# Two-part score products for the heads, page-wise keys for the samples and two banks for branch products in a hybrid decoder step

## The chip, the cores and the metric

The kernel runs on one core of one Trainium2 chip. A core has TensorE (PE, matrix products, written to the eight banks of PSUM), VectorE (DVE), ScalarE (ACT), GpSimd (POOL) and SyncE (SP, which issues most of the transfers). The engines run beside each other, each takes its own instructions in order, and they wait for each other through semaphores. The metric is the device time of one execution in microseconds.

## What is computed

One step of a decoder layer, for 512 new prompt tokens and for 8 sequences of 4 sampled tokens each with 1024 cached positions (544 tokens in all). Everything comes in and goes out as float32. Cut to what matters:

```python
# one projection of the normed input gives all of these
q_a, kv_a, q_i, k_i, w_i, q_b, kv_b, gates = _project(_rmsnorm(x), w_in, pos)
# A: sparse attention, 8 heads on 2 key groups, the 256 best keys by an indexer score
s = einsum('btcgd,btncd->btcgn', q_a, keys_of(idx)) * HEAD_DIM ** -0.5 ; p = softmax(s)
# B: stick-breaking attention, 8 heads
z = einsum('bthd,bshd->bhts', q_b, k_b) * HEAD_DIM ** -0.5
a = exp(log_sigmoid(z) + sum of log(1 - sigmoid(z)) over the later keys) ; o_b = a @ v_b
merged = gates[0] * (o_a @ w_br_a) + gates[1] * (o_b @ w_br_b)
h = x + merged @ w_o ; h = h + _ffn(_rmsnorm(h)) ; y = _rmsnorm(h)
```

## The kernel before

The tokens are the columns of the products (two halves of 256 and 288 columns), so an activation is a tile of 128 features by 544 tokens. Dense products are made of two-part numbers: a value is split into a high part in the format float32r and the rest (`wh`, `wl` for weights, `xh`, `xl` for activations), and three products `wh*xh + wl*xh + wh*xl` are added in PSUM (L502, in `pieces`). For the weights the high part is an ACT copy (L113) and the low part a POOL subtraction (L117). The heads' and samples' products take plain float32, which PE issues as two rows of the trace for each product.

In order of time: the input is normed and turned; the indexer's rows, the stick-breaking queries, keys and values are projected (`V["wide"]`, banks in turn); from about 178 us three streams run beside each other in `beside`, each a generator that yields its estimated cost, the next step being taken from the stream that is least far along its given total (`S_COST`, `H_COST`, `D_COST`): *samples* (`sb_sample`, then `dsa_sample`), *heads* (`staged`: stick-breaking, then sparse, each over 4 pairs of heads j and 4 row blocks i, so 32 units) and *dense* (remaining projections and gates, then `branch_b`, which makes the first `NB` = 5 of 8 row blocks of the stick-breaking branch product). From about 485 us on there are only branch products, then the gates, `w_o` and the FFN. Within that program order a planner with a simulated timeline places each engine's instructions.

PSUM has 8 banks: `mm` 1, `z` 2, `acc` 1, `tp` 2, `ts` 2. A unit of the heads (`sb_first`, `dsa_first`) takes one tile `z` of two banks, one for each head of the pair, and makes both heads' scores side by side, each in a 64-row half of the array (`scores_of`, L859). In the stick-breaking branch a mask product (L935) is added, ACT makes two sigmoids (L938, L939), DVE a scan and a product (L941, L942); in the sparse branch DVE adds the mask (L972) and ACT takes the exponential. Queries and keys of a pair are loaded in `sb_load` and `dsa_load`, at i = 1 and i = 0 of the pair before.

In `sb_sample` the cached keys of four sequences at a time come by pages of 128 positions (`rows_of_page`, 12 tiles), are turned (L1030) and copied out of PSUM (`out_of`); `scores` (L1038) makes the logits of two pages in `acc`, which are copied to `zr`, from which `weights` takes the sigmoids. Outside the wide stages `pieces` uses the bank `mm` alone, and ACT copies it out (L538 for projections, L1281 for branch products) into `rowy`, of which there are two tiles.

## Time and profile before

| | us |
|---|---|
| median of 3 runs (range) | 994.39 (994.14 to 999.39) |
| profiled execution | 998.12 |
| its span, first to last instruction | 996.0 |
| PE busy in the span | 939.0 (94%) |
| DVE, ACT, POOL busy | 642.2, 452.5, 298.3 |

A row of the timeline gives the start and the duration of an instruction, or of several alike in a row (x4). Matmuls are pipelined and their ends are modelled, so the duration of a PE row runs on into the next row; what a product costs in a dense stretch is read from its start to the next start.

### The profile page before, as it was taken

How to read it: one execution, taken by the hardware profiler on the slowest of the kernel's cores; microseconds unless marked ns; L12 is line 12 of the kernel's file. 1: busy time of each engine (PE TensorE's matmuls, PEld its weight loads, DVE VectorE, ACT ScalarE, POOL GpSimd, SP SyncE). 2: the span in 40 equal slices, each digit the busy share in tenths (PEclk: the TensorE clock that was granted, in tenths of full speed). 3: DMA queues.
4: the chain of work that ended last, by engine and by line, in shares of the span. 5: the costliest groups of instructions: out<-in, count | busy, mean ns of one | idle time of the engine just before them, and what ended most of it. 6: DMA issues, size and time to landing. Idle time of an engine off the chain costs nothing.

```text
span 996.0 us, 19681 instructions
## 1 busy us (share of the span) xinstructions
PE 939.0 (94%) x7412; PEld 846.9 (85%) x7412; DVE 642.2 (64%) x1238; ACT 452.5 (45%) x889; POOL 298.3 (30%) x260
## 2 busy tenths in 40 slices
PE   5989999889899999999978999999999999999995
PEld 4989999766478775877768999989999999999995
DVE  4465999475565574443204585987778788875874
ACT  6214543455335434444555355544444445442453
POOL 3544343211221321223238456222322232201331
PEclk9989999989999999999999999999999999999998
DMA  9673454857787698415267845123333431235212
GB/s 262 179 191 107 132 159 140 263 164 216 243 256 229 201 305 261 151 61 223 88 209 231 229 116 146 46 64 107 86 102 89 123 90 41 66 93 160 83 48 90
DMA packets 180408, 150.67 MB, mean 151 GB/s; under 512 B 12378, under 2 KB 147354, under 8 KB 179290
## 3 DMA queue, kind: packets, MB, share of 16 engines
q1 hardware_dynamic: 175146, 134.45, 45.1%
q0 software_dynamic: 1872, 10.75, 3.1%
q10 hardware_dynamic: 3296, 4.23, 1.4%
q8 instruction: 58, 0.95, 0.4%
q14 instruction: 36, 0.29, 0.1%
HBM read 126.43 MB, written 17.56 MB: 145 GB/s over the span
## 4 chain that ended last, share of the span: by engine, by line
PE 66%; DVE 10%; DMA 8%; issue 3%; POOL 2%; ACT 2%; SPq 1%; ACTq 0%; DVEq 0%; POOLq 0%
PE mm L502 14%; PE ffB L1562 9%; PE ffC L1562 5%; PE ffA L1562 5%; PE ts L502 3%; PE ts L1647 3%; PE ts L1030 2%; PE z L859 2%; PE acc L502 2%; PE z L502 2%; PE dnB L1740 2%; PE tp L866 2%; POOL wl L117 2%; PE tp L875 1%; PE acc L1647 1%
## 5 line engine op out<-in xcount | busy, mean ns | idle before, releaser
L117 POOL TENSOR_TENSOR wl<-wst,wh 128x512 fp32r<-128x512 f32 (+2 forms) x136 | 161.3, 1209 | 307.4 <-ACT wh L113 293.1
L502 PE MATMUL mm<-xh,wh 128*128 128x256 f32 (+2 forms) x484 | 148.0, 306 | 9.4 <-ACT rowy L1281 7.1
L502 PE MATMUL mm<-xh,wl 128*128 128x256 f32 (+2 forms) x484 | 143.7, 297 | 1.3 <-POOL wl L117 1.3
L502 PE MATMUL mm<-xl,wh 128*128 128x256 f32 (+2 forms) x484 | 143.9, 297 | 0.0
L237 POOL TENSOR_TENSOR wl<-wst,wh 128x512 fp32r<-128x512 f32 (+1 forms) x48 | 66.7, 1410 | 174.0 <-ACT wh L234 157.9
L502 PEld LDWEIGHTS mm<-xh,wh 128*128 128x128 f32 (+1 forms) x484 | 93.4, 193 | 21.7 <-ACT rowy L1281 8.9
L113 ACT ACTIVATE wh<-wst 128x1024 fp32r<-128x1024 f32 (+3 forms) x83 | 75.1, 906 | 55.8 <-PE ts L1647 23.5
L502 PEld LDWEIGHTS mm<-xh,wl 128*128 128x128 f32 (+1 forms) x484 | 93.1, 192 | 7.7 <-issue 6.1
L502 PEld LDWEIGHTS mm<-xl,wh 128*128 128x128 f32 (+1 forms) x484 | 93.2, 192 | 2.0 <-issue 1.6
L234 ACT ACTIVATE wh<-ws 128x1024 fp32r<-128x1024 f32 (+1 forms) x55 | 54.9, 998 | 79.2 <-PE ffB L1562 29.2
L239 DVE TENSOR_TENSOR wl<-ws,wh 128x1024 fp32r<-128x1024 f32 (+1 forms) x55 | 66.4, 1208 | 5.5 <-ACT wh L234 5.5
L234 ACT ACTIVATE wh<-wst 128x1024 fp32r<-128x1024 f32 (+1 forms) x34 | 34.8, 1024 | 23.6 <-PE ffB L1562 15.5
L1030 PE MATMUL ts<-ident,kb 128*128 128x128 f32 x256 | 39.1, 282 | 2.1 <-DMA kb<-in_cache_kv_b 1.1
L843 ACT ACTIVATE kk<-ts 128x512 f32<-128x512 f32 x43 | 25.1, 600 | 31.4 <-PE ts L1030 31.0
L237 POOL TENSOR_TENSOR wl<-raw,wh 128x384 fp32r<-128x384 f32 x14 | 14.2, 1039 | 80.3 <-ACT wh L234 64.3
L538 ACT ACTIVATE rowy<-mm 128x256 f32<-128x256 f32 (+1 forms) x40 | 15.8, 394 | 49.3 <-PE mm L502 41.5
L1030 PEld LDWEIGHTS ts<-ident,kb 128*128 128x128 f32 x256 | 29.2, 144 | 7.7 <-DMA kb<-in_cache_kv_b 1.3
L211 DVE TENSOR_TENSOR ws<-wst 128x1024 f32<-128x1024 f32 (+1 forms) x11 | 21.4, 1947 | 19.9 <-DMA wst<-in_w_ffn_up 18.8
L1647 PE MATMUL ts<-actp,wh 128*128 128x288 f32 x160 | 34.1, 295 | 0.0
L941 DVE TENSOR_TENSOR_SCAN g<-g,z 128x128 f32<-128x128 f32 (+3 forms) x32 | 26.1, 816 | 11.8 <-ACT z L939 9.2
L938 ACT ACTIVATE g<-z 128x128 f32<-128x128 f32 (+3 forms) x32 | 13.9, 436 | 37.0 <-PE z L935 34.3
L502 PE MATMUL z<-xh,wh 128*128 128x288 f32 (+2 forms) x92 | 28.1, 305 | 1.8 <-DVE hT L1379 1.8
(485 smaller groups left out, 3075.4 us busy)
## 6 DMA issues: line engine op xcount, KB each, us to landing
wst<-in_w_in SPq DMA_DIRECT2D x38, 512.0 KB, 4.2
kb<-in_cache_kv_b SPq DMA_DIRECT2D x64, 256.0 KB, 3.8
vb<-in_cache_kv_b SPq DMA_DIRECT2D x64, 256.0 KB, 4.9
wst<-in_w_ffn_gate SPq DMA_DIRECT2D x40, 256.0 KB, 3.0
wst<-in_w_ffn_up SPq DMA_DIRECT2D x40, 256.0 KB, 3.4
wst<-in_w_ffn_down SPq DMA_DIRECT2D x16, 320.0 KB, 3.1
gate_d<-rowy SPq DMA_DIRECT2D x16, 272.0 KB, 2.1
gt<-gate_d SPq DMA_DIRECT2D x16, 272.0 KB, 3.6
```

Of the source, the lines that this page charges most:

```text
L113: self.nc.scalar.activation(h, st, AF.Copy)
L117: self.nc.gpsimd.tensor_sub(l[:, k], st[:, k], h[:, k].bitcast(F32))
L211: v.tensor_add(t, a("A21"), a("A22"))
L234: self.nc.scalar.activation(h, src, AF.Copy)
L237: self.nc.gpsimd.tensor_sub(l[:, g], src[:, g], h[:, g].bitcast(F32))
L239: self.nc.vector.tensor_sub(l, src, h.bitcast(F32))
L502: nc.tensor.matmul(ps, ww[:, k, :m], aa[:, k, hs], start=(k == 0 and p == 0), stop=(k == nk - 1 and p == 2))
L843: nc.scalar.activation(dst, ps, AF.Copy)
L941: nc.vector.tensor_tensor_scan(gr, gr, z[:, :n], 1.0, OP.mult, OP.bypass)
L1030: nc.tensor.transpose(tp[:, (2 * j + pg) * P:(2 * j + pg + 1) * P], raws[pg][:, (2 * jj + j) * P:(2 * jj + j + 1) * P], ident)
L1562: nc.tensor.matmul(ps[:, g], ww[:, g, k, :], aa[:, k, :], start=(first and k == 0 and p == 0), stop=(k == 3 and p == 2), skip_group_check= ...
L1647: nc.tensor.matmul(ps, ww[:, k - ks[0], :], aa[:, hs], start=(k + p == 0), stop=(k + 1 == DOWN[-1][-1] and p == 2))
```

## The change

The tile `z` becomes two tiles of one bank. A head's query tile holds its high part in the first 64 rows and its low part in the other 64, its key tile holds the keys' high parts in both halves and, in a second plane, their low parts in both; two products over all 128 rows with float32r operands then give the four partial products. The parts are made on chip from a raw tile that is loaded twice, once into each half. Loads for the next pair are issued at i = 3, head by head. The samples' keys are turned by single pages, the logits of half a sequence's keys (four pages) stay in `acc`, and the sigmoids read it there. Branch products in the overlapped stretch take `mm` and `acc` in turn. The bank lists of the other stages are adapted to the two `z` tiles, and costs, totals and buffer counts change.

```diff
-H_COST = 80
-D_COST = 174
+H_COST = 88
+D_COST = 185
-KV_C = 6
-KH_B = 8
+KV_C = 4
+KH_B = 6
-    zb2 = lambda: V["psum"].tile([P, 2, 512], F32, tag="z", name="z", bufs=1)
-    zb = lambda: zb2()[:, 0, :]
+    zb = lambda: bank("z", 2)
...
-    px_banks = cycle([lat, lts, lat, lts, zb, acc])
+    px_banks = cycle([lat, lts, lat, lts, zb, zb, acc])
...
-    V["banks"], many = cycle([mm, zb, acc, lts]), cycle([mm, zb, acc, lts, lts])
+    V["banks"], many = cycle([mm, zb, zb, acc]), cycle([mm, zb, zb, acc, lts, lts])
...
-            ps = (next(V["banks"]) if V["wide"] else mm)()[:m, :hs.stop - hs.start]
+            ps = (next(V["banks"]) if V["wide"] or nk == 4 else mm)()[:m, :hs.stop - hs.start]
...
-    def scores_of(zs, q, k, i):
+    def both_halves(pool, tag, src):
+
+        t = pool.tile([P, *src.shape[1:]], F32, tag=tag, name=tag, bufs=1)
+        for e in range(2):
+            nc.sync.dma_start(t[half_of(e)], src)
+        return t
+
+    def query_parts(pool, src, name):
+
+        t = both_halves(pool, "qraw", src)
+        q = pool.tile([P, T], F32R, tag="qq", name=name, bufs=2)
+        nc.scalar.activation(q, t, AF.Copy)
+        nc.vector.tensor_sub(q[64:], t[64:], S(q[64:]))
+        return q
+
+    def key_parts(pool, src, tag, bufs):
+
+        t = both_halves(pool, "kraw", src)
+        k = pool.tile([P, 2, T], F32R, tag=tag, name=tag, bufs=bufs)
+        nc.scalar.activation(k[:, 0], t, AF.Copy)
+        nc.gpsimd.tensor_sub(k[:, 1], t, S(k[:, 0]))
+        return k
 
+    def scores_of(z, q, k, i):
         n = (i + 1) * P
-        in_turn([lambda e=e: nc.tensor.matmul(zs[:, e, :n], q[half_of(e), i * P:(i + 1) * P], k[half_of(e), :n], start=True, stop=True,
-                                              skip_group_check=True) for e in range(2)])
+        for v in range(2):
+            nc.tensor.matmul(z[:, :n], q[:, i * P:(i + 1) * P], k[:, v, :n], start=(v == 0), stop=(v == 1))
...
     def sb_first(j, i):
-        if i == 1 and j < 3:
-            sb_load(j + 1)
-        q, kk, _ = V["sbq", j]
         n = (i + 1) * P
-        zs = zb2()
-        scores_of(zs, q, kk, i)
...
         for e in range(2):
-            z = zs[:, e]
+            z = zb()
+            scores_of(z, *V["sbq", 2 * j + e], i)
+            if i == 3 and j < 3:
+                sb_load(2 * j + 2 + e)
...
-        if i == 0 and j < 3:
-            dsa_load(j + 1)
...
+            z = zb()
+            scores_of(z, V["dsaq", 2 * j + e], kaa[j // 2], i)
+            if i == 3 and j < 3:
+                dsa_load(2 * j + 2 + e)
...
-        def scores(g, c, jj, kks, z):
-            for j in range(2):
-                side_by_side(lambda n4: nc.tensor.matmul(
-                    z[quarter(n4), :2 * P], qb[:, 4 * g + n4, 2 * jj + j, :], kks[n4][:, j, :],
-                    start=(jj + j == 0), stop=(jj + j == 2), skip_group_check=True))
+        def scores(g, c, kks, z):
+
+            in_turn([lambda j=j, n4=n4: nc.tensor.matmul(
+                z[quarter(n4), c * P:(c + 1) * P], qb[:, 4 * g + n4, j, :], kks[n4][:, j, :],
+                start=(j == 0 and c == 0), stop=(j == 3), skip_group_check=True) for j in range(4) for n4 in range(3, -1, -1)])
+
+        def logits(g, half):
+
+            z, ahead = acc(), []
+            for c in range(4):
+                kks = []
+                for n4 in range(4):
+                    kks.append(keys(rows_of_page(0, 4 * g + n4, 4 * half + c)))
+                    yield 0.45
+                    if n4 == 1 and ahead:
+                        scores(g, *ahead.pop(), z)
+                        yield 1.1
+                ahead.append((c, kks))
+            scores(g, *ahead.pop(), z)
+            yield 1.1
+            return z
...
-            nc.scalar.activation(r[:, lo:hi], zr[:, lo:hi], AF.Sigmoid, scale=-1.0)
-            nc.scalar.activation(zr[:, lo:hi], zr[:, lo:hi], AF.Sigmoid)
+            nc.scalar.activation(r[:, lo:lo + 512], z, AF.Sigmoid, scale=-1.0)
+            nc.scalar.activation(zr[:, lo:lo + 512], z, AF.Sigmoid)
+            if half:
+                nc.scalar.activation(r[:, PAST:], zr[:, PAST:], AF.Sigmoid, scale=-1.0)
+                nc.scalar.activation(zr[:, PAST:], zr[:, PAST:], AF.Sigmoid)
...
-    V["wide"] = False
+    V["wide"], V["banks"] = False, cycle([mm, acc])
...
-        kaa, va = dp.tile([P, 2, T], F32, name="kaa"), dp.tile([P, 4, P], F32, name="va")
-        for e in range(2):
-            nc.sync.dma_start(kaa[half_of(e)], ka_d.rearrange("(c d) t -> d c t", c=2))
+        kaa, va = [key_parts(dp, ka_d[half_of(c)], "kaa", 2) for c in range(2)], dp.tile([P, 4, P], F32, name="va")
...
-    V["banks"] = cycle([mm, lts, acc, lts])
+    V["banks"] = cycle([mm, zb, zb, acc])
```

## Rows read from the trace of the kernel before

**Rows 1.** The page's chain that ended last, share of the span by engine.
```profile
PE 66%; DVE 10%; DMA 8%; issue 3%; POOL 2%; ACT 2%; SPq 1%; ACTq 0%; DVEq 0%; POOLq 0%
```

**Rows 2.** Windows: busy us by engine (instructions), then granted clock, DMA share, GB/s.
```profile
178.00:330.00 152.00, 140.10 (x1163) 102.10 (x1164) 88.16 (x232) 71.42 (x161) 30.97 (x23) 0.97 0.74 229
485.00:530.00 45.00, 34.91 (x300) 28.94 (x300) 6.97 (x18) 23.79 (x46) 16.58 (x21) 1.00 0.54 170
...
200.00:225.00 25.00, 21.33 (x168) 15.42 (x167) 17.92 (x43) 14.17 (x32) 2.51 (x2) 0.86 0.51 166
```

**Rows 3.** Timeline of PE (start, duration, what): paired scores L859 and neighbours.
```profile
188.93 0.28 PE L502 MATMUL mm<-xh,wh 128*128 128x256 f32 x1
189.14 0.70 PE L859 MATMUL z<-kk,qq 64*128 64x256 f32 x4
...
243.02 1.13 PE L859 MATMUL z<-kk,qq 64*128 64x512 f32 x4
...
251.44 0.49 PE L859 MATMUL z<-kk,qq 64*128 64x128 f32 x4 [0.40 <-PE acc L1038]
...
433.17 1.13 PE L859 MATMUL z<-kaa,qqa 64*128 64x512 f32 x4
434.23 0.40 PE L502 MATMUL mm<-xh,wh 128*128 128x288 f32 x1
434.47 0.29 PE L502 MATMUL mm<-xh,wl 128*128 128x288 f32 x1
434.60 0.29 PE L502 MATMUL mm<-xl,wh 128*128 128x288 f32 x1
...
438.27 0.49 PE L859 MATMUL z<-kaa,qqa 64*128 64x128 f32 x4
438.70 0.76 PE L1006 MATMUL ts<-ident,sr 128*128 128x128 f32 x5
```

**Rows 4.** Timeline of PE: the prompt indexer's two-part scores, 256 and 512 keys.
```profile
88.17 0.28 PE L831 MATMUL tp<-kll,qs 128*128 128x256 f32 x1
88.29 0.30 PE L502 MATMUL z<-xh,wh 128*128 128x288 f32 x1
...
126.31 0.39 PE L831 MATMUL tp<-kll,qs 128*128 128x512 f32 x1
126.54 0.29 PE L502 MATMUL ts<-xl,wh 128*128 128x288 f32 x1
```

**Rows 5.** Timeline of PE: samples' key products L1038, samples' value products L1182.
```profile
324.04 1.07 PE L1038 MATMUL acc<-kk,qb 128*32 128x256 f32 x16
325.05 1.13 PE L859 MATMUL z<-kk,qq 64*128 64x512 f32 x4
...
493.89 1.08 PE L1182 MATMUL acc<-kav,pT 128*32 128x128 f32 x32
494.90 0.38 PE L502 MATMUL mm<-xl,wh 128*128 128x256 f32 x1
```

**Rows 6.** Timeline of POOL and of ACT: passes over 128x512.
```profile
482.69 1.29 POOL L1260 TENSOR_TENSOR xl<-rowy,xh 128x512 fp32r<-128x512 f32 x1 [6.76 <-ACT xh L1259]
...
498.79 0.62 ACT L113 ACTIVATE wh<-wst 128x512 fp32r<-128x512 f32 x1
```

**Rows 7.** Waits of PE (us in total, times, longest): 178 to 480, then 485 to 530.
```profile
PE z L859 <- DVE b L942: 2.6, 3, 2.0
...
PE z L935 <- DVE b L942: 1.4, 2, 1.2
...
PE mm L502 <- ACT rowy L1281: 7.1, 8, 1.5
```

**Rows 8.** The chain in order of time (start, us, what), branch products' end.
```profile
523.25 3.33 DMA rowy<-od
```

**Rows 9.** DMA issues, 170 to 490 us: count, KB each, median us to landing.
```profile
kk<-k_d SPq DMA_DIRECT2D x4, 256.0 KB, 4.4
...
qqa<-qa_d SPq DMA_DIRECT2D x4, 256.0 KB, 6.1
```

More of the change, by code (lines that the diff above doesn't have):

```diff
@@ L907, in weights_tiles, with sb_load @@
         return [pool.tile([P, i + 2, 2, P], F32, tag=f"pt{i}{e}", name="pt", bufs=2) for e in range(2)]
-    def sb_load(j):
+    def sb_load(hd):
         hp = V["hp"]
-        tiles = [hp.tile([P, T], F32, tag=n, name=n, bufs=2) for n in ("qq", "kk")]
-        for t, src in zip(tiles, (q_d, k_d)):
-            nc.sync.dma_start(t, src[j])
-        v = hp.tile([P, 4, P], F32, tag="vs", name="vs", bufs=2)
-        nc.sync.dma_start(v, v_d[j])
-        V["sbq", j] = (*tiles, v)
+        j, r = hd // 2, half_of(hd % 2)
+        if hd % 2 == 0:
+            V["v", j] = hp.tile([P, 4, P], F32, tag="vs", name="vs", bufs=2)
+            nc.sync.dma_start(V["v", j], v_d[j])
+        V["sbq", hd] = query_parts(hp, q_d[j, r], "qq"), key_parts(hp, k_d[j, r], "kk", 2)
     def sb_first(j, i):
@@ L921, in sb_first @@
             sb_load(0)
[L922 to L924 removed]
+            sb_load(1)
         n = (i + 1) * P
[L926 to L927 removed]
         if "g" not in V:
@@ L1023, in rows_of_page, with keys @@
             return raw
-        def keys(raws, jj):
+        def keys(raw):
             tp = lts()
-            for j in range(2):
-                for pg in range(2):
-                    nc.tensor.transpose(tp[:, (2 * j + pg) * P:(2 * j + pg + 1) * P],
-                                        raws[pg][:, (2 * jj + j) * P:(2 * jj + j + 1) * P], ident)
-            kk = sp_.tile([P, 2, 2 * P], F32, tag="kk", name="kk", bufs=KH_B)
-            out_of(kk, tp.rearrange("p (j k) -> p j k", j=2))
-            return kk
@@ L1036, in scores @@
-        def scores(g, c, jj, kks, z):
-            for j in range(2):
-                side_by_side(lambda n4: nc.tensor.matmul(
-                    z[quarter(n4), :2 * P], qb[:, 4 * g + n4, 2 * jj + j, :], kks[n4][:, j, :],
-                    start=(jj + j == 0), stop=(jj + j == 2), skip_group_check=True))
-        def logits(g, zr, cc):
-            ahead = []
-            def done(c, jj, kks):
-                if jj == 0:
-                    V["zs"] = acc()
-                scores(g, c, jj, kks, V["zs"])
-                if jj:
-                    out_of(zr[:, c * 2 * P:(c + 1) * 2 * P], V["zs"][:, :2 * P])
-            for c in cc:
-                raws = {}
-                for jj in range(2):
-                    kks = []
-                    for n4 in range(4):
-                        if jj == 0:
-                            raws[n4] = [rows_of_page(0, 4 * g + n4, pg) for pg in (2 * c, 2 * c + 1)]
-                        kks.append(keys(raws[n4], jj))
-                        yield 0.45
-                        if n4 == 1 and ahead:
-                            done(*ahead.pop())
-                            yield 1.2
-                    ahead.append((c, jj, kks))
-            done(*ahead.pop())
-            yield 1.2
@@ new lines, in keys @@
+            for j in range(4):
+                nc.tensor.transpose(tp[:, j * P:(j + 1) * P], raw[:, j * P:(j + 1) * P], ident)
+            kk = sp_.tile([P, 4, P], F32, tag="kk", name="kk", bufs=KH_B)
+            out_of(kk, tp.rearrange("p (j k) -> p j k", j=4))
+            return kk
+        def scores(g, c, kks, z):
+            in_turn([lambda j=j, n4=n4: nc.tensor.matmul(
+                z[quarter(n4), c * P:(c + 1) * P], qb[:, 4 * g + n4, j, :], kks[n4][:, j, :],
+                start=(j == 0 and c == 0), stop=(j == 3), skip_group_check=True) for j in range(4) for n4 in range(3, -1, -1)])
@@ L1118, in sb_sample @@
             for half in (1, 0):
-                yield from logits(g, zr, (2 * half + 1, 2 * half))
-                weights(half, zr, r, a)
+                z = yield from logits(g, half)
+                weights(half, z, zr, r, a)
                 yield 1.0
@@ L1304, in heads @@
         dsa_load(0)
+        dsa_load(1)
         yield D_LAT
```

13 lines of the change are left out of this document (4 added, 9 removed).

## The prediction

> **What bounds the kernel now.** I read the page's chain first [rows 1]: TensorE (PE) carries 66% of it, DVE 10%, DMA 8%. An engine that carries two thirds of the chain sets the time through two things, how densely its instructions are issued and where it stands still. So I went on to the windows of the stretch that the change touches [rows 2]. From 178 to 330 us (stick-breaking heads beside samples beside dense rows) PE is busy 140.10 of 152.00 us; from 485 to 530 us (the branch products) 34.91 of 45.00 us; DMA has a share of 0.74 in the first. Busy is no good measure of what PE could give back, because a row's duration overlaps the next row. The measure I use is the start-to-start spacing of PE rows in the timeline, read for the old score products and for their nearest relatives [rows 3 to 5]. The waits that PE itself suffers come last: they say what goes if a wait goes. The reader should see two things: the stretch is a queue of issues with few holes, so an edit is worth what it shortens in issue time, plus the holes that it closes; and the dense holes are at the end, in the branch products.
>
> **Heads' scores.** Now one unit (a pair of heads, i+1 key blocks) is 4 issues, two for each head, side by side in 64-row halves of the array. From start to the next start such a unit takes 1.06 us with 512 keys (433.17 to 434.23) and 0.43 us with 128 (438.27 to 438.70) [rows 3]; in even steps between them, 0.85 and 0.64 us. There are 8 units of each size (4 pairs in each of the two branches), so 8 x (1.06 + 0.85 + 0.64 + 0.43) = 23.8 us. The change makes it 4 issues of the two-part form over all 128 rows. That form runs already, in the prompt's indexer: 0.23 us with 512 keys and 0.12 us with 256 [rows 4], so 0.175 us with 384 in between. Four of each are 0.92, 0.70 and 0.48 us: 8 x (0.14 + 0.15 + 0.16) = 3.6 us saved. With 128 keys no row shows the form. From below it is half the 256-key issue, 0.06 us (0.24 a unit, 1.5 us saved in all 8); from above it falls to the speed of the plain float32 product, two issues of 0.107 us each [rows 3], 0.86 a unit, 3.4 us lost. I take the 0.43 of today, since the other small product with a full weight load in hand is the 256-key one at 0.12, and four of those are 0.48. Term: **-3.6** (-5.1 to -0.2).
>
> The Trainium skill ("TensorE: Matmul & The Clock Gate", section on LDWEIGHTS) prices a weight load by its 128 columns at 128/1.2 = 107 ns, which would be an estimate of 0.43 us for the four issues with 128 keys and leave the sum as it is. The same page (Part 3, row and column tiling) speaks against this change: products of few rows run concurrently when placed in different row groups, so giving up the pairing should cost. By that rule alone a unit of 512 keys would double to 2.1 us and the term would be +24 instead of -3.6; no row here shows it, because the full-height form with 512 keys is timed at 0.23 us an issue.
>
> **Entering and leaving the half-height form.** An ordinary dense product is followed after 0.13 us; the last one ahead of a paired score is followed after 0.21 (188.93 to 189.14, a 256-column one that normally takes 0.12) and the first behind it after 0.24 (434.23 to 434.47) [rows 3]. The indexer's two-part products are followed by a dense one without such a gap [rows 4]. So each pair of heads costs up to 0.09 + 0.11 = 0.20 us more at its edges, 32 x 0.20 = 6.4 us, all of which can go. But many units have a transpose or a samples' product as neighbour, which keeps an edge of its own. I take a third: **-2** (-6.4 to 0).
>
> **Samples' keys by pages.** Today 16 issues over 256 columns take 1.01 us (324.04 to 325.05), and there are 16 such groups. Afterwards there are 16 pages of 32 issues over 128 columns. The samples' value products in the other branch have just that form: 32 issues in 1.01 us (493.89 to 494.90) [rows 5]. So **0**. Eight evictions of 128x256 go, and four small sigmoids come, off the path. The logits now stay in the `acc` bank from the first page of a half to its two sigmoids, so the next half's first product waits behind them, and everything queued behind it on PE waits too: 2 halves in each of 2 groups, two sigmoids of the size of the 0.62 us ACT pass [rows 6] each time, less the eviction that was waited for before. Bound -1 to +2, taken 0 because the dense rows are there to fill. Page tiles fall from 12 to 10 and key tiles from 8 to 6. That is free as long as 10 pages cover SP's blockings, and costs below if not.
>
> **Two banks for the heads' logits.** They were one tile of two banks; they become two tiles. PE waited 2.6 us at the scores and 1.4 us at the mask product for DVE's last read of the other head [rows 7]. With separate tiles head 1 no longer waits for head 0's chain: **-3** (-4.0 to 0). The spare bank also serves the dense products of the early part and the start; PE hardly waits for a bank there, 0 (-1 to 0).
>
> **Branch products.** In the overlapped stretch each half (12 issues, 1.4 to 1.6 us by the 0.12 and 0.13 spacings) goes into `mm`, and the next waits until ACT has copied it out: 7.1 us in 8 waits, longest 1.5 [rows 7]. With `mm` and `acc` in turn, a half runs while the other is copied, and a wait as long as the longest is hidden by a half's own 1.4 us. What is late next is the way of the last heads' outputs: `rowy` loads of 3.33 us [rows 8] that share their buffers with the branch products' outputs, ahead of the tile `hT`. They follow the last copy and so move ahead with it. I take **-6** (-7.1 to -3).
>
> **The parts made on chip.** Each head of the stick-breaking branch now needs 4 loads, two ACT copies (0.62 us each), a DVE and a POOL subtraction (1.29 us on POOL [rows 6]; DVE unpriced for this, between 0 and that 1.29, taken 0.6); each head of the sparse branch 2 loads, one copy and one DVE subtraction; the two key groups one copy and one POOL pass. ACT gets 26 copies, 16 us, DVE about 10 us, POOL 10 x 1.29 = 13 us, spread over 300 us in which none of them is the bound; POOL's passes stand in line ahead of the weights' low parts, on which dense products wait. **+1** (0 to +3). On SP the change adds 38 issues, and with one raw tile the second head's load blocks SP until the first head's raw tile was read. Loads were issued three or four units ahead and are now issued one unit ahead. In the sparse branch a load lands after 6.1 us [rows 9]; with 0.62 and 0.6 that is 7.3 us for the first head and 14.6 for the second, against a lead of 5.1 us (433.17 to 438.27 [rows 3]): 9.5 us late, three times. In the other branch 4.4 [rows 9] + 0.62 + 1.29 = 6.3, twice 12.6, against 8.4 us from 243.02 to 251.44 [rows 3]: 4.2 us late, three times. So the heads' stream slips by up to 3 x 9.5 + 3 x 4.2 = 41 us in all. On PE the slip is hidden by dense and samples' products as long as the planner puts them ahead of the late scores; where it has not, PE stands, and the pages queued behind on SP with it. Between 0 and 41 I take a tenth, **+4**, since the planner does know loads and takes other streams meanwhile.
>
> **Sum.** -3.6 - 2 + 0 - 3 - 6 + 1 + 4 = -9.6 us. It is made against the profiled execution, whose span is 996.0 us and time 998.12; the median of the three runs is 994.39, 3.7 below. The edits act in the same stretch in both, so 994.4 - 9.6 = **984.8 us**.
>
> **The rivals.** *Late loads win (slower).* One mechanism: SP and the one raw tile. If half of the 41 us falls on PE, the sum is -13.6 + 20.5 = +6.9, 1001 us; from 13.6 us on PE (a third) the change is no gain. For it: the lead shrinks to one unit, and DMA has a share of 0.74 already [rows 2]. Against it: only dense products stand between, and there are enough of them. *The gain is small (no change).* The branch stretch is set by the `rowy` loads and weights rather than by the copies, so 3 of the 6 us come back, and the 128-key form runs at float32 speed, +3.4: -9.6 + 3 + 3.4 = -3.2, 991 us. For it: these loads end last behind the products [rows 8]. That the two-part form doesn't do what it says falls into this case. *More (faster).* In 200 to 225 us the granted clock is only 0.86 [rows 2], in a stretch where PE stood behind DVE. If these holes close, the clock may stay at its upper level of 2.4 GHz: 28% of 25 us were then at 1.2 GHz, 7 us, of which half, 3.5 us, comes back; with no loss by loads, -9.6 - 4 - 3.5 = -17, 977 us.
>
> **Chances.** Forecast (979 to 989) 0.48, more 0.17, small gain or none 0.22, late loads 0.13. A measurement of this kernel can tell about 0.5%, 5 us, from no change, so faster means under 989.4: 0.65; within: 0.22; slower: 0.13. The range 974 to 998 takes in the rivals of a larger and of a small gain, and the near half of the slow one.
>
> **What would show it.** Score rows of 128 rows with about 0.23 us spacing at 512 keys; no 0.2 us gaps at their edges; the waits of `mm` for the copy L1281 gone and branch products in `mm` and `acc`; from 200 to 225 us a higher clock. Wrong: PE or the score rows waiting for the raw tiles' DMA or for ACT, DVE or POOL making parts; page products waiting for `kb` or `vb`; 128-key issues of 0.2 us; `acc` waits in the samples' products that were not there.

## The result and the profile after

The changed kernel takes 1001.48 us, the kernel before 994.8 us in the runs beside it: a ratio of 1.0063 (95% interval 1.0050 to 1.0076). The forecast was 984.8 us, faster by 1%; the change is slower by 0.6%, and the time lies outside the range of 974 to 998. It is the time that the rival of late loads gave (1001 us).

The page after, PE's line of the busy times and the chain by engine:

```profile
span 1000.7 us, 20343 instructions
...
PE 929.3 (93%) x7668; PEld 861.1 (86%) x7668; DVE 653.9 (65%) x1252; ACT 470.2 (47%) x917; POOL 317.3 (32%) x270
...
PE 50%; DMA 9%; DVE 8%; issue 3%; ACT 2%; POOL 2%; SPq 2%; ACTq 0%; DVEq 0%; POOLq 0%
```

PE is busy 9.7 us less than before (939.0), which is the size of the gain that was forecast (9.6), and yet the span is 4.7 us longer (996.0 to 1000.7). So the work did get shorter, and PE stands still more. That the fall is as large as the forecast is chance: only 5.6 of the 9.6 us were meant as shorter issues. Where PE stands still, is read from the stretch that the change touches: from the first samples' product (`acc<-knew,qb`) to ACT's first copy into `hT`, the tile of the last branch products. In windows of that stretch (length, PE busy, clock, DMA share, GB/s), the kernel before:

```profile
177.50:528.60 351.10, 327.38 (x2689) 0.98 0.64 205
```

and the changed kernel, with the windows that answer to [rows 2] below it:

```profile
168.59:534.64 366.05, 323.49 (x2975) 0.97 0.68 208
...
178.00:330.00 152.00, 136.07 (x1289) 108.07 (x1289) 96.42 (x248) 74.00 (x168) 42.47 (x32) 0.98 0.79 236
485.00:530.00 45.00, 37.78 (x333) 31.69 (x329) 8.31 (x19) 25.45 (x49) 17.20 (x22) 1.00 0.55 177
200.00:225.00 25.00, 20.00 (x190) 15.64 (x179) 20.07 (x49) 16.36 (x39) 5.09 (x4) 0.93 0.79 226
```

The stretch begins 8.9 us sooner and is 14.9 us longer. Busy time in it falls by 3.9 us although 33 more dense issues lie in it (1152 for 1119; at 0.13 us each 4.3 us), so like for like by 8.2. Length less busy, which I call idle, grows from 23.7 to 42.6 us, by 18.9. In 178 to 330 us the idle time of [rows 2] was 11.9 us and is now 15.9.

The waits of PE (us in total, times, longest), 178 to 480 us, then 485 to 540, beside [rows 7]:

```profile
PE mm L501 <- ACT rowy L537: 10.4, 4, 7.0
...
PE z L881 <- DVE b L961: 3.2, 3, 2.4
PE z L881 <- ACT kk L874: 2.2, 1, 2.2
...
PE mm L501 <- ACT hT L1387: 7.4, 1, 7.4
...
PE acc L501 <- ACT rowy L1288: 0.9, 2, 0.5
PE mm L501 <- ACT rowy L1288: 0.7, 2, 0.5
```

The branch products' waits for their copy did go, 7.1 us to 0.9 + 0.7. Two holes of 7.0 and 7.4 us stand in their place. The first, in the timeline of PE (start, duration, what, idle before):

```profile
427.57 0.33 PE L881 MATMUL z<-kaa,qqa 128*128 128x128 f32 x1
434.92 0.61 PE L501 MATMUL mm<-xh,wh 128*128 128x288 f32 x1 [7.03 <-ACT rowy L537]
435.33 0.44 PE L501 MATMUL mm<-xh,wl 128*128 128x288 f32 x1
435.57 0.44 PE L501 MATMUL mm<-xl,wh 128*128 128x288 f32 x1
```

in that of ACT:

```profile
423.56 0.63 ACT L866 ACTIVATE qqa<-qraw 128x512 fp32r<-128x512 f32 x1 [3.01 <-DMA qraw<-qa_d]
...
433.97 0.63 ACT L866 ACTIVATE qqa<-qraw 128x512 fp32r<-128x512 f32 x1 [8.04 <-DMA qraw<-qa_d]
434.50 0.37 ACT L537 ACTIVATE rowy<-mm 128x256 f32<-128x256 f32 x1
```

in that of SP, which issues the loads:

```profile
418.40 1.12 SPq L859 DMA_DIRECT2D qraw<-qa_d  x2
...
424.94 1.10 SPq L859 DMA_DIRECT2D qraw<-qa_d  x2
```

and in windows of 10 us:

```profile
420.00:430.00 10.00, 7.51 (x62) 6.39 (x59) 5.00 (x18) 2.40 (x6) 3.18 (x4) 1.00 0.97 310
430.00:440.00 10.00, 5.08 (x27) 4.97 (x27) 2.00 (x7) 2.90 (x9) 0.00 (x0) 0.66 0.22 75
```

Read together: the second head's raw query is issued at 424.94, when the one raw tile has been read for the first head (copy at 423.56, its low part taken by DVE until 424.91). Its second half lands at 433.88, 8.9 us later; DMA has a share of 0.97 from 420 to 430 us. ACT takes its instructions in order and stands at the copy L866 for 8.04 us; behind it is the copy L537, which empties the bank `mm`; and on that waits a dense product, the kind of work that was meant to cover late loads.

What keeps DMA busy there is not the heads' own traffic. POOL issues two gathers of the samples' cached rows (`kav`) at 423.57 and 424.83. From 425 to 434 us the software queue that carries them (packets, MB, share of 16 engines) stands beside the ordinary queue, and below it is the late half's load in the chain of the changed kernel (start, us, what):

```profile
424.83 0.94 POOL L421 DMA_INDIRECT kav<-in_cache_kv_a,rowid  x1 [0.30 <-DMA wst<-in_w_in]
...
q0 software_dynamic: 288, 2.10, 67.6%
q1 hardware_dynamic: 255, 0.31, 10.4%
...
425.44 8.44 DMA qraw<-qa_d
```

The second hole, in the chain in order of time (start, us, what), the line that answers to [rows 8] at its head:

```profile
523.51 4.74 DMA rowy<-od
...
528.94 0.70 DVE xl L1267
...
529.66 2.96 DMA rowy<-od
...
533.35 1.27 POOL xl L1267
...
534.64 0.39 ACT hT L1387
```

Three outputs of the sparse heads are loaded at the end (`heads_out`, issued at 521.91, 523.51 and 529.66), through the two `rowy` tiles that the branch products' outputs use as well. The third is issued 0.02 us after the subtraction that frees its tile (528.94 + 0.70). Before, PE waited 1.8 us for `hT`, now 7.4.

### The profile page after: what moved, and what is told of

The parts are those of the page before. It is cut to its first block, busy times and chain, and to the rows that moved or that the text cites. A ratio compares the mean times of both kernels' runs of the same rounds, so it can differ in the third digit from the quotient of the medians.

```text
span 1000.7 us, 20343 instructions
## 1 busy us (share of the span) xinstructions
PE 929.3 (93%) x7668; PEld 861.1 (86%) x7668; DVE 653.9 (65%) x1252; ACT 470.2 (47%) x917; POOL 317.3 (32%) x270
## 4 chain that ended last, share of the span: by engine, by line
PE 50%; DMA 9%; DVE 8%; issue 3%; ACT 2%; POOL 2%; SPq 2%; ACTq 0%; DVEq 0%; POOLq 0%
PE mm L501 9%; PE ffB L1568 8%; PE ffC L1568 5%; PE ffA L1568 5%; PE z L1653 3%; DMA qraw<-qa_d 2%; PE dnB L1746 2%; POOL wl L117 2%; PE acc L1653 2%; DMA vb<-in_cache_kv_b 2%; PE ts L1045 1%; PE mm L1653 1%; PE dnC L1746 1%; DMA rowy<-od 1%; PE ts L501 1%
## 5 line engine op out<-in xcount | busy, mean ns | idle before, releaser
L501 PE MATMUL mm<-xh,wh 128*128 128x256 f32 (+2 forms) x460 | 141.9, 308 | 21.1 <-ACT rowy L537 10.9
L501 PE MATMUL mm<-xl,wh 128*128 128x256 f32 (+2 forms) x460 | 137.7, 299 | 0.1
L501 PE MATMUL mm<-xh,wl 128*128 128x256 f32 (+2 forms) x460 | 136.3, 296 | 0.0
L501 PEld LDWEIGHTS mm<-xh,wh 128*128 128x128 f32 (+1 forms) x460 | 89.2, 194 | 31.1 <-ACT rowy L537 12.1
L501 PEld LDWEIGHTS mm<-xl,wh 128*128 128x128 f32 (+1 forms) x460 | 89.1, 194 | 4.6 <-issue 2.5
L501 PE MATMUL z<-xh,wh 128*128 128x256 f32 (+2 forms) x168 | 50.6, 301 | 0.0
L501 PE MATMUL z<-xh,wl 128*128 128x256 f32 (+2 forms) x168 | 50.5, 301 | 0.0
L501 PE MATMUL z<-xl,wh 128*128 128x256 f32 (+2 forms) x168 | 49.6, 297 | 0.0
L234 ACT ACTIVATE wh<-wst 128x1024 fp32r<-128x1024 f32 (+1 forms) x34 | 34.8, 1024 | 22.8 <-PE ffB L1568 14.6
L842 ACT ACTIVATE kk<-ts 128x512 f32<-128x512 f32 x47 | 27.8, 596 | 21.6 <-PE ts L1045 18.4
L501 PEld LDWEIGHTS z<-xh,wh 128*128 128x128 f32 (+1 forms) x168 | 33.0, 196 | 0.1
L501 PEld LDWEIGHTS z<-xh,wl 128*128 128x128 f32 (+1 forms) x168 | 33.0, 196 | 0.1
```

The source lines that it names most:

```text
L234: self.nc.scalar.activation(h, src, AF.Copy)
L501: nc.tensor.matmul(ps, ww[:, k, :m], aa[:, k, hs], start=(k == 0 and p == 0), stop=(k == nk - 1 and p == 2))
L842: nc.scalar.activation(dst, ps, AF.Copy)
```

## The experiments

Ratios are to the kernel before, from runs beside it, with 95% intervals. The last columns are from one profiled execution each: the stretch from the first samples' product to `hT`, PE busy and idle in it, dense issues in it, and when the samples' last output is turned (`ts<-ident,oa`), with which their stream ends. One execution alone moves by some us: E6, E12, E13, E14 and E16 have the PE order of the kernel before up to 177 us, and their stretches begin between 172.4 (E13) and 179.5 us (E6) for 177.5, with a clock of 1.00 and 0.91 in the first 100 us for 0.93.

| kernel | ratio | stretch | busy | idle | dense | samples end |
|---|---|---|---|---|---|---|
| before | 1 | 351.1 | 327.4 | 23.7 | 1119 | 498.3 |
| changed | 1.0063 (1.0050-1.0076) | 366.0 | 323.5 | 42.6 | 1152 | 505.8 |
| E1 changed, early queries | 0.9987 (0.9967-1.0006) | 363.3 | 328.9 | 34.3 | 1152 | 502.5 |
| E2 changed, own tiles at the end | 0.9945 (0.9919-0.9971) | 351.4 | 317.5 | 33.9 | 1120 | 503.2 |
| E3 changed, old totals | 0.9936 (0.9907-0.9965) | 350.4 | 323.4 | 26.9 | 1137 | 493.9 |
| E4 changed, float32 scores | 0.9936 (0.9915-0.9957) | 352.7 | 336.1 | 16.6 | 1137 | 494.4 |
| E5 before, two z tiles | 0.9963 (0.9939-0.9988) | 355.1 | 337.3 | 17.8 | 1133 | 492.5 |
| E6 before, branch in two banks | 0.9965 (0.9946-0.9985) | 347.4 | 322.9 | 24.5 | 1119 | 499.3 |
| E7 = E1 + E2 + E3 | 0.9852 (0.9814-0.9891) | 339.9 | 315.3 | 24.6 | 1088 | 491.2 |
| E8 = E4 + own tiles | 0.9906 (0.9869-0.9943) | 345.5 | 328.4 | 17.2 | 1089 | 496.8 |
| E9 = E1 + E2 | 0.9926 (0.9898-0.9953) | 346.9 | 319.0 | 27.9 | 1117 | 499.2 |
| E10 = E1 + E3 | 0.9849 (0.9798-0.9901) | 349.8 | 322.8 | 27.0 | 1137 | 493.4 |
| E11 = E2 + E3 | 0.9898 (0.9858-0.9938) | 340.4 | 318.5 | 21.9 | 1098 | 491.8 |
| E12 before, pages | 0.9880 (0.9825-0.9936) | 345.3 | 324.9 | 20.4 | 1121 | 480.3 |
| E13 before, pages and branch | 0.9818 (0.9788-0.9848) | 337.4 | 319.5 | 17.9 | 1119 | 479.0 |
| E14 = E13 + own tiles | 0.9798 (0.9768-0.9828) | 328.8 | 313.4 | 15.4 | 1085 | 480.8 |
| E15 changed, no pages | 0.9914 (0.9881-0.9948) | 349.4 | 317.3 | 32.1 | 1152 | 492.1 |
| E16 = E12, fewer tiles | 0.9892 (0.9851-0.9933) | 338.9 | 319.2 | 19.7 | 1119 | 483.4 |
| E17 = E15 + own tiles | 0.9834 (0.9807-0.9861) | 341.6 | 315.8 | 25.9 | 1135 | 492.5 |
| E18 = E15 + E1 + E2 + E3 | 0.9879 (0.9844-0.9914) | 346.5 | 316.1 | 30.4 | 1094 | 500.7 |

### E1 to E3: the two holes and the totals

E1 loads the sparse heads' raw queries at i = 0 of the pair before, into two raw tiles (shared with the raw keys), and leaves the parts where they were:

```diff
+        if i == 0 and j < 3:
+            dsa_raw(2 * j + 2)
+            dsa_raw(2 * j + 3)
-        t = both_halves(pool, "qraw", src)
+        if t is None:
+            t = both_halves(pool, "qraw", src)
```

> Change as it is, but the raw query tiles of the sparse heads are loaded at i = 0 of the pair before, into two raw tiles. Theory A (late loads: ACT stands in order behind a raw load, PE behind ACT): ACT's wait for the sparse raw loads, 12.8 us in the changed kernel, falls under 3 us, the PE hole of 7.0 us for the copy of `mm` goes, the granted clock of that stretch returns to 1.0; 8 to 10 us less, about 992 us, level with before or a little faster. Theory B (the end of the branch products is what counts, and it moves with the samples' stream): 0 to 2 us less, about 1000 us.

996.57 us. ACT's wait for the sparse raw queries and PE's for `hT`:

```profile
ACT qqa L867 <- DMA qraw<-qa_d: 1.6, 2, 1.1
...
PE mm L501 <- ACT hT L1395: 8.3, 1, 8.3
```

That wait of ACT was 12.8 us in the changed kernel, and the 7.0 us hole is gone with it: theory A, a little short of its 8 to 10 us. So the first hole is the late load, and it cost some 7.6 thousandths, 7.6 us. The last two raw queries are now issued at 412.1 and 414.3 us, ahead of the gathers (420.6 and 421.8) instead of beside them. The hole ahead of `hT` stays.

E2 gives the outputs that are loaded at the end three tiles of their own:

```diff
-        t = row("y")
+        t = pool.tile([P, T], F32, tag="ho", name="ho", bufs=3) if pool else row("y")
```

> Change as it is, but the heads' outputs that are loaded at the end of the overlapped stretch get three tiles of their own and no longer share `rowy` with the branch products. Theory B (the PE hole of 7.4 us ahead of the tile hT is the chain of three loads through two shared tiles): the hole falls to 2 us or less, 5 us less in time, about 996 us. Theory A: the hole ahead of hT stays or moves, under 2 us less, about 999 us or more.

991.55 us. PE no longer waits for `hT` at all; the first hole is where it was:

```profile
430.59 0.61 PE L501 MATMUL mm<-xh,wh 128*128 128x288 f32 x1 [7.01 <-ACT rowy L537]
```

So the second hole is the chain of loads through shared tiles. The first stands beside the gathers again (`kav` issued at 419.03 and 420.28, the raw query at 420.6). Its removal gave 11.8 thousandths, more than the 7.4 us of the hole and twice what theory B expected; the rest is not accounted for.

E3 puts the totals of the heads' and the dense stream back:

```diff
-H_COST = 88
-D_COST = 185
+H_COST = 80
+D_COST = 174
```

> Change as it is with H_COST and D_COST back at 80 and 174. Theory C (the new totals pull heads and dense rows ahead of the samples, whose stream now ends at 506 us rather than 499, and the branch products start late): the samples end 5 us or more earlier and the time falls by 3 to 7 us, about 996 us. Theory A: the order of the streams is of no account, the late loads only move to another place: within 2 us of the changed kernel, about 1000 us.

990.13 us, 12.7 thousandths gained by two numbers that change no instruction, only the order; theory C had 3 to 7 us. The hole ahead of `hT` halves, the late loads bite elsewhere and less:

```profile
PE mm L501 <- ACT rowy L546: 5.2, 2, 4.6
PE mm L501 <- ACT hT L1387: 3.7, 1, 3.7
```

Larger totals make the two streams look less far along, so they are taken ahead of the samples; with the old ones the samples end at 493.9 us for 505.8.

### E4 to E6: the parts alone

E4 is the changed kernel with the scores as joint float32 products, without parts and raw loads, and with the old totals and buffer counts; E5 is the kernel before with only the two one-bank tiles and the bank lists; E6 with only the branch products' two banks. E5 and E6:

```diff
-        zs = zb2()
-        scores_of(zs, q, kk, i)
+        zs = [zb(), zb()]
+        scores_of(zs, q, kk, i)
```

```diff
-            ps = (next(V["banks"]) if V["wide"] else mm)()[:m, :hs.stop - hs.start]
+            ps = (next(V["banks"]) if V["wide"] or nk == 4 else mm)()[:m, :hs.stop - hs.start]
-    V["wide"] = False
+    V["wide"], V["banks"] = False, cycle([mm, acc])
```

> Before with the two z tiles and their bank lists, page-wise keys and two banks for branch products, but the heads' scores as paired float32 products loaded as before, and the old totals and buffer counts. Theory A (the heads' parts cost the loss, the rest gains): 8 to 13 us less than the kernel before, about 984 us. Theory D (the page-wise keys or the two banks cost it): no faster than before, 994 us or more.

> The kernel before with only the two one-bank score tiles and the bank lists that go with them; scores stay float32 and joint, the samples' keys and the branch products stay as before. Theory (the bank lists give a gain in the early stage that the prediction put at nothing): the samples' stretch begins some 4 us sooner than the 177.5 us of the kernel before, the wait z <- DVE b falls from 4.0 to about 3, and the time falls by 3 to 6 us: 991 to 994 beside 996.7. Rival (the early gain belongs to another part, as the shorter planner totals): first samples product at 177 to 178, time within 1.5 us of the kernel before.

> The kernel before with only the branch products taking two banks in turn. Theory (the waits for the copy go, but the hT copies behind them wait for a chain of three loads through two shared row tiles, so the gain turns up as a hole ahead of the FFN): PE's waits on the copy of L1281 fall from 7.1 to about 1.5, the wait mm <- ACT hT grows from 1.8 to 5 or more, and the time stays within 2 us of 996.7. Rival (the term of the prediction, the gain moves ahead): hT wait stays near 2, time 5 to 7 us lower, 990 to 992.

E4 took 990.86, E5 991.64, E6 991.99 us. E4 lies between its two theories. E5 is in the range of its theory (991 to 994), its first samples' product at 171.3 us; at the same clock of 0.97 in the first 100 us E12 without the bank lists has it at 174.7, so the lists give some 3.4 us there, which the prediction put at nothing. But E5 and E4 have a side effect that I had not foreseen. PE in E5:

```profile
188.82 1.12 PE L858 MATMUL z<-kk,qq 64*128 64x512 f32 x2
189.88 0.23 PE L934 MATMUL z<-mb,identb 128*128 128x128 bf16 x1
...
190.81 1.07 PE L1037 MATMUL acc<-kk,qb 128*32 128x256 f32 x16
191.81 1.12 PE L858 MATMUL z<-kk,qq 64*128 64x512 f32 x2
```

With a tile for each head the planner issues the two heads apart, and one head alone takes 1.06 us (188.82 to 189.88), as long as the pair of [rows 3]. The score rows, from start to next start, sum to 38.6 us for 27.0 before, and busy time in E5's stretch is 9.9 us higher (1.8 of it for 14 more dense issues). That is the rule of the Trainium skill ("TensorE: Matmul & The Clock Gate", Part 3: Packing small matmuls), by which products of few rows run concurrently in different row groups; the trace agrees for the half-height form (1.06 us for one or for two). So E4 doesn't price the two-part scores cleanly: it lost the pair.

E6 shows its theory's mechanism, but not its time. Waits on the copy go, `hT` comes late:

```profile
PE mm L502 <- ACT hT L1381: 5.9, 1, 5.9
...
PE mm L502 <- ACT rowy L1281: 1.1, 1, 1.1
```

Its ratio says 3.5 us (1.5 to 5.4) gained, between theory and rival: about half of the 6 us of the prediction is given back at the shared tiles.

### E7 to E11: repairs together

> The changed kernel with both stretches of idle time taken away: the sparse heads' raw queries loaded one pair of heads ahead into two tiles (the edit of the first experiment), the last heads' outputs in tiles of their own (the second), and the planner's old totals of 80 and 174 (the third). Theory (the change's own gains of 9.7 us of PE time are real and were lost in these holes): waits of ACT on the raw queries near 2 us, no idle stretch of PE above 4 us from 250 to 540, time 980 to 986, ratio 0.984 to 0.990. Rival (the holes move on: the same idle time turns up at another transfer or wait): 988 to 992, no better than the second or third experiment, with idle time of the stretch near 40 us.

> The fourth experiment's kernel (all of the change but the two-part scores, the scores staying joint float32 products) with the last heads' outputs in tiles of their own. Theory (its 3.8 us hole ahead of the hT copies closes too): 986 to 989, ratio 0.990 to 0.993; beside the run with both holes closed this gives what the two-part scores are worth once their loads are not late: the prediction's 4.6 us (terms for cadence, edges and parts) would make that run 4 to 5 us faster than this one. Rival (the two-part form is worth about 1 us, as its rows in the changed kernel sum to 26.1 us for 27.0): the two runs within 2 us.

> The changed kernel, its planner totals left at 88 and 185, with the sparse raw queries loaded one pair ahead and the last heads' outputs in own tiles. Theory (the totals cost time only through the two holes, so once these are closed they change nothing): within 2 us of the run that has the old totals as well, 979 to 983, ratio 0.983 to 0.987. Rival (larger totals cost of their own, by putting the heads' last pieces and the samples' end later and leaving less dense work for the waits in between): 985 to 990, ratio 0.988 to 0.994, with samples ending later than 497 us.

> Early raw queries and old totals, the shared row tiles at the end left as in the changed kernel. Theory (the chain of loads through the shared tiles costs 3 to 4 us still, as the third experiment's hole of 3.7 us ahead of the hT copies shows): 984 to 987, ratio 0.988 to 0.991. Rival (the hole moves with the earlier samples' end and costs nothing): 979 to 982, as with own tiles.

> Own tiles for the last heads' outputs and old totals, the raw queries' loads left late, through one raw tile, as in the changed kernel. Theory (late loads cost PE 3 to 4 us also in the old order, as the third experiment's hole of 3.35 us in front of a product behind the copy of the raw query shows): 984 to 987, ratio 0.987 to 0.991. Rival (there the wait is covered by other dense work): within 2 us of the run with early loads, 979 to 983.

E7 took 980.8 us, in the range of its theory; the stretch is 26 us shorter than in the changed kernel, some 8 us of it because 64 dense issues (0.13 us each) now stand behind it:

```profile
170.80:510.67 339.87, 315.32 (x2910) 0.98 0.71 219
```

Alone, the three repairs gave 7.6, 11.8 and 12.7 thousandths, together 21.1 and not 32.1: they take the same idle time in part. E9 (987.58) falls to its rival: with both holes closed the new totals still cost 7.4 thousandths (2.7 to 12.1), so they act through the order as such and not through the two holes only. E10 (981.56) falls to its rival too, within its wide interval: with early loads and old totals the own tiles gave nothing measurable. E11 (985.83) is in the range of its theory, 4.6 thousandths behind E7, but the two intervals overlap: that late loads cost time in the old order too is not shown. E8 (986.84) agrees with its own; that E7 is 5.4 thousandths faster (barely clear of the noise) can't be put down to the two-part scores, as E8 has lost the pair.

### E12 to E15: the pages, with the pair kept

E12 is the kernel before with only the page-wise `keys`, `scores`, `logits` and `weights`; E13 adds E6's edit, E14 the own tiles of E2; E15 is the changed kernel with the old samples' code, its tile counts as changed. E12, and E15 the other way round:

```diff
-                yield from logits(g, zr, (2 * half + 1, 2 * half))
-                weights(half, zr, r, a)
+                z = yield from logits(g, half)
+                weights(half, z, zr, r, a)
```

> The kernel before with only the samples' keys taken page by page and their logits kept in PSUM. Prediction: a term of nothing, -1 to +2 us, so 995 to 998 beside a kernel before of 996. Rival (the page-wise form frees the engines that empty PSUM, or moves the samples' end, by enough to see): 990 to 993. Rival on the other side (its 16-issue groups ran 0.1 us longer each in the changed kernel and its page tiles, fewer than before, made PE wait 3.4 us for values instead of 0.8): 998 to 1001.

> The kernel before with page-wise keys and branch products in two banks; the paired float32 scores and their one two-bank tile z stay. Theory (the gains of these two parts alone, about 10 and 3.5 us, add up, because one acts from 178 to 260 us and the other at the end): 980 to 983 beside a kernel before of 995, ratio 0.984 to 0.988. Rival (the end is set by the chain of loads through the shared row tiles, so a sooner branch product brings nothing on top): as with pages alone, 985 to 988.

> The same with the last heads' outputs in tiles of their own. Theory (pages, branch and tail hold all that the change has to give, and the two-part scores with their two one-bank tiles bring nothing): 976 to 981, at least as fast as the changed kernel with both holes closed and the old totals (980.8). Rival (the two-part scores and the two tiles bring some 5 us of their own): 984 to 988, slower than that kernel.

> The changed kernel with the samples' keys and logits done as before (two pages at a time, logits copied out of acc). Theory (page-wise keys and the two tiles for the heads' logits close the same holes of the early stretch, 178 to 260 us, so that in the changed kernel the pages bring nothing): 999 to 1004, ratio 1.003 to 1.009. Rival (the pages bring about 10 us wherever they stand): 1008 to 1014.

E12 took 985.81 us, faster than any of its expectations. Windows of the kernel before:

```profile
0.00:100.00 100.00, 85.42 (x588) 81.33 (x589) 53.81 (x111) 39.08 (x84) 42.17 (x48) 0.93 0.67 184
168.00:260.00 92.00, 82.22 (x695) 60.15 (x693) 55.49 (x143) 45.21 (x99) 15.45 (x15) 0.96 0.64 200
```

and of E12:

```profile
0.00:100.00 100.00, 84.59 (x608) 80.81 (x609) 55.48 (x119) 39.71 (x86) 42.01 (x48) 0.97 0.70 188
168.00:260.00 92.00, 86.59 (x875) 65.80 (x874) 52.60 (x134) 45.40 (x99) 16.14 (x14) 1.00 0.78 246
```

From 168 to 260 us PE is busy 4.4 us more, DVE 2.9 us less, and the granted clock is 1.00 for 0.96: the stretch that ran partly at 1.2 GHz [rows 2] runs at 2.4 GHz. That is the mechanism of the rival "more", reached by a part to which the prediction gave nothing. Some 3 us of the single execution belong to the first 100 us and not to the pages; the interval of the ratio says 6 to 17 us in all. How much of that is the pages' own and how much the new order that they bring, E12 alone can't say.

E13 took 978.16 us, below both its ranges, and E14 976.09, in the range of its theory (the step between them, 2 thousandths, is within the noise): pages and branch add up, and without two-part scores the kernel is as fast as any that has them. E15 took 986.62 us: in the changed kernel the pages do not gain 10 us, they cost 15, which neither expectation allowed. Waits of E15 that answer to those of the changed kernel:

```profile
ACT qqa L866 <- DMA qraw<-qa_d: 2.4, 2, 1.2
...
PE mm L501 <- ACT hT L1396: 7.3, 1, 7.3
```

The hole ahead of `hT` is the same, the one at 428 us is not there, and the samples end at 492.1 for 505.8. In this order the gathers (407.26 and 408.52) fall between two raw queries (issued at 405.2 and 422.3).

### E16 to E18: why the pages cost in the changed kernel

E16 is E12 with the changed kernel's tile counts, E17 is E15 with the own tiles, E18 is E15 with all three repairs:

```diff
-KV_C = 6
-KH_B = 8
+KV_C = 4
+KH_B = 6
```

> The kernel with page-wise keys alone, with 4 page tiles of the samples' own and 6 key tiles as in the changed kernel, instead of 6 and 8. Theory (the pages gain when there are tiles enough to run ahead and lose when there are not: with 6 key tiles there is none to spare, since the products of four sequences are issued after the second of the next four): most of the gain of pages alone goes, 993 to 998 beside a kernel before of 996. Rival (tiles don't matter, the order of the streams does): 984 to 988 as with all tiles.

> The changed kernel without the page-wise keys and with the last heads' outputs in tiles of their own. Theory (the 7.3 us hole ahead of the hT copies that stood in the run without pages closes, and nothing takes its place): 978 to 981, ratio 0.982 to 0.985. Rival (the hole moves on to another transfer): 983 to 987.

> The changed kernel without the page-wise keys and with all three repairs (early raw queries, own tiles at the end, old totals). Theory (pages cost in the changed kernel whatever the rest, since the raw tiles took the room of their page and key tiles): faster than the run with both holes closed and pages (980.8) by 5 us or more, 968 to 976. Rival (with the repairs the pages cost nothing, the 15 us were part of the same holes): 978 to 983.

E16 took 986.0 us, its rival: the tiles that the raw tiles displaced are not the reason. E17 took 979.43 us, as its theory had it: the hole ahead of `hT` closes and nothing takes its place. E18 took 984.99 us, slower than both its expectations; E7, which has the pages, took 980.8, but their intervals overlap. Its longest hole, on PE:

```profile
343.66 0.66 PE L1029 MATMUL ts<-ident,zr 128*128 128x128 f32 x2 [7.07 <-DVE zr L1107]
```

on ACT:

```profile
340.96 0.63 ACT L875 ACTIVATE kaa<-qraw 128x512 fp32r<-128x512 f32 x1 [6.75 <-DMA qraw<-ka_d]
341.49 0.64 ACT L1103 ACTIVATE zr<-zr 128x544 f32<-128x544 f32 x1
```

It is the first hole again at another load: ACT stands 6.75 us at the copy of a raw key, behind it is the samples' `zr`, on that DVE, on that PE. DMA has a share of 0.90 from 330 to 350 us, and again two `kav` gathers (327.92 and 329.24) were issued just ahead of the raw keys (331.1 and 332.3). In E7, where the pages stay, ACT's waits for raw keys of that branch sum to 2.3 us.

What is settled: the late raw loads and the end chain are real and named, and the totals cost by themselves. The three longest waits of ACT for a raw tile of the sparse branch (8.0 in the changed kernel, 7.9 in E2, 6.8 us in E18) all stand beside two `kav` gathers. That the gathers make these loads late is read from the traces and not isolated: no run moves them alone, and waits of 5 us stand without them (E3, E11). That the two-part scores bring nothing here is read from their rows (below) and from E14 (0.9798), which has none of the parts and is no slower than E17 (0.9834), which has them; no run swaps the scores alone and keeps the pair.

What stays open is the step from E12 to E15. E16 rules out the tile counts, E17 the end chain (without pages it is 11 thousandths faster than E2, where the chain is closed too). The late sparse queries are at most a part: E9 has the pages, with both long holes closed, and is still 9 thousandths slower than E17 (0.9926 and 0.9834). With the old totals as well, no cost of the pages is left (E7 and E18, within the noise, though E18 has a hole of its own). So the cost hangs on the pages together with the new totals, that is on the order of the three streams; the samples end at 499.2 in E9 for 492.5 in E17, but why that costs 9 us is not shown.

## Why the prediction was wrong

**The sum.** Of the -9.6 us, -5.6 were PE's issues (scores and edges), -9 waits that close (z banks and branch) and +5 parts and late loads. PE's busy time fell by 9.7 us in the span, and like for like by 8.2 in the stretch. What the prediction lacked is idle time: +18.9 us where its terms had closed holes of 9 us and opened one of 4.

**Heads' scores, -3.6.** Mis-sized. The score rows, from start to next start and without the idle time inside, sum to 26.1 us for 27.0 (the prediction had 23.8, from two rows), so -0.9; without the pages (E15) to 25.0, where the float32 pair in E13 has 25.3. By keys they take 8.7 us for 9.5 (512), 7.2 for 8.0, 5.5 for 5.7 and 4.7 for 3.7 (128). The 0.23 us an issue of [rows 4] was right for products behind their like. What failed is that a unit is four such issues in a row. With a tile for each head the planner issues the two heads apart, as in E5 (12 of 14 groups with 512 keys are one head's two products), and in 11 of the 14 groups the first product takes 0.31 to 0.34 us to the next start, in ten of them behind a transpose or another product that is not a dense one. So a group of two takes 0.55 us on average for 0.46, and four in a row 1.02, where four times 0.23 are 0.92 and [rows 3] has 1.06:

```profile
420.24 1.18 PE L881 MATMUL z<-kaa,qqa 128*128 128x512 f32 x4
421.26 0.28 PE L501 MATMUL mm<-xh,wh 128*128 128x256 f32 x1
421.37 0.28 PE L501 MATMUL mm<-xh,wl 128*128 128x256 f32 x1
```

**Edges, -2.** The dense product behind goes on at its ordinary 0.11 us, so the edge that fell on the next row is gone. The heads' transposes and value products, which often stand beside score rows, take 38.8 us for 43.2 (E15 beside E13: 38.7 for 41.9), a dense product 0.141 us in both (0.139 in E13 and E15). If all of that is edge, rows and edges together came to 3.5 to 5.2 us, near the -5.6, with more from the edges and less from the rows than forecast. The +24 us that the prediction worked out from Part 3 of the Trainium skill's page did not come (26.1 us in all). The rule there is about products of few rows; E5 shows it for them, while the two-part form fills all 128 rows.

**Samples' pages, 0.** The failed step of largest size. Price of the issues: 18.4 us busy before, 20.3 after, small as I had it; PE waited for `acc` 0.8 us, behind DVE's addition into `zr`, and not for the sigmoids. What I had no term for is the order: alone the pages gave 12 thousandths (E12), in the changed kernel they cost 15 (E15).

**Two banks for the logits, -3.** PE's waits for DVE's last read were 4.0 us [rows 7]. With the two tiles alone (E5) 0.2 us is left, as forecast; in the changed kernel 3.2 us. The bank lists gave 3.4 us at the start (E5), where I had written 0.

**Branch products, -6.** Half right. The waits for the copy went as forecast (7.1 to 1.6). The step that failed is the sentence that the loads "follow the last copy and so move ahead with it": they share two tiles with the outputs they follow, and three loads, each with a subtraction behind it, wait for one another. PE waited 5.6 us more for `hT`, closing that chain gave 11.8 thousandths (E2), and alone the edit gave 3.5 instead of 6 us (E6).

**Parts and late loads, +1 and +4.** The mechanism was right, its place was not. From the first head's issue (418.40) to the end of the second's copy (434.60) it took 16.2 us, where I had worked out 14.6 with the subtraction. But I had SP and the pages stand behind it, with dense products as cover. It was ACT that stood, with a dense product's copy behind it, so the cover itself stopped. E1 prices it at 7.6 us. The rival's 1001 us is met in number only: it wanted 20.5 us from this mechanism alone.

**Totals.** The prediction said that costs, totals and buffer counts change and had no term for it. E3 says 12.7 thousandths, as much as the pages within the intervals.

**The clock.** The rival "more" was right about [rows 2]: from 200 to 225 us the clock is 1.00 in E5, E12 and E13 for 0.86 before and 0.93 in the changed kernel. But it does not sort the kernels by time: over 168 to 260 us E13 and E14, the fastest, have 0.98 like the changed kernel. That E13 takes 978 us, the rival's 977, is met in number only.

**Adding terms.** E5, E6 and E12 gave 3.7, 3.5 and 12.0 thousandths, and E4, which holds all three, 6.4, some 13 less than their sum (about 7 of noise). The lost pairs don't explain it, as E5's 3.7 has that loss in it already (9.9 us of busy time, less 1.8 for 14 more dense issues). One part of it is that E5 and E12 close the same holes. In the window of E12 above, E5 has:

```profile
168.00:260.00 92.00, 88.65 (x710) 61.02 (x710) 61.06 (x157) 48.95 (x111) 16.28 (x13) 1.00 0.65 202
```

The idle time of PE there is 9.8 us before, 5.4 in E12 and 3.4 in E5, so what the two close together (4.4 and 6.4 us) is more than there was. The rest stays open.

## What to carry to other kernels

Before calling dense work the cover of a late load, follow who empties the dense work's bank: an engine that takes its queue in order and waits for the load in front of that copy turns the cover into part of the stall. Look at what else is on the DMA engines when such a load is issued: here it was another stream's gather. Price the order as well as the work: a planner's totals, and a tile shared by two streams, moved this kernel by more than every product that was made shorter. And test parts alone and in company, since the same edit gave 12 thousandths in one order and cost 15 in another.

## What the runs showed of the hardware

A product that fills half of the array's rows takes as long alone as two of them side by side: 1.06 us at 512 keys either way (E5 and [rows 3]).

A small load can take twice its usual time beside a gather. Loads of the sparse raw queries in the changed kernel (count, KB, median us to landing):

```profile
qraw<-qa_d SPq DMA_DIRECT2D x16, 128.0 KB, 4.2
```

The half that ended the first hole took 8.44 us, while the gathers' queue had 67.6% of the 16 engines' time and the ordinary loads' 10.4%.

After the idle time of 7.0 us PE went on at the lower level of its clock: 0.24 us from start to start for 288 columns (435.33 to 435.57) where a dense stretch has 0.13, and 0.66 granted from 430 to 440 us. That hole so cost more than its length.

And the clock of the first 100 us lay between 0.91 and 1.00 in six kernels with the same PE order there (0.91 in E6, 0.93 before, 0.97 in E12, 1.00 in E13), with the start of the stretch 7.1 us sooner in E13 than in E6. One profile alone does not settle a few us.
